# Page gathers of a decoder step issued one by one along the weight half tiles of the first stage; window-cache copies placed in the last stage

## The chip, the cores and the metric

The kernel runs on one core of one Trainium2 chip. The metric is device time in microseconds (us) of one execution. The kernel before took 1522.66 us, the median of three runs (1521.82 to 1527.60).

The engines are PE (TensorE, matmuls, with weight loads shown as PEld), ACT (ScalarE), DVE (VectorE), POOL (GpSimd) and SP (SyncE, here only a DMA queue). Each engine works through its own instructions in order; semaphores order them against each other.

## The reference

One step of a hybrid decoder layer: a half-step feed-forward network, a mixing part with two groups of heads, a second half-step feed-forward network, and a final norm. Prompt (512 rows) and decode rows (8 sequences x 4) go through the same projections. Cut to what matters here:

```python
def ffn_half(x, g, wg, wu, wd):
    h = rms_norm(x, g)
    return x + 0.5 * ((jax.nn.silu(h @ wg) * (h @ wu)) @ wd)

def compress(rows, pe, w1, w2):
    n, length = rows.shape[:2]
    blk = rows.reshape(n, length // CMP_BLOCK, CMP_BLOCK, N_KV_NSA, HEAD_DIM) + pe[:, None, :]
    hid = jnp.einsum('nbcgd,cde->nbge', blk, w1)
    return jax.nn.gelu(hid) @ w2

# in nsa_sample, for the K and the V pool
past = pool[page_table].reshape(n, PAST_LEN, N_KV_NSA, HEAD_DIM)
...
# in reference, for layer l
xp = ffn_half(xp, ffn1_norm[l], ffn1_wg[l], ffn1_wu[l], ffn1_wd[l])
xs = ffn_half(xs, ffn1_norm[l], ffn1_wg[l], ffn1_wu[l], ffn1_wd[l])
...
xp = ffn_half(xp, ffn2_norm[l], ffn2_wg[l], ffn2_wu[l], ffn2_wd[l])
xs = ffn_half(xs, ffn2_norm[l], ffn2_wg[l], ffn2_wu[l], ffn2_wd[l])
# in nsa_sample: the updated window buffers
kw_all = jnp.concatenate([cache_win_k, kw], axis=1)
return ..., kw_all[:, -wb:], vw_all[:, -wb:]
```

D_MODEL is 1024, D_FF 2816. The decode step reads 16 pages of 128 rows for each of 8 sequences, found through a page table: 128 page slots. Each is multiplied by the compression weights w1 (`hid`). The window buffers of the 8 sequences (512 rows) move up by 4 rows, so that 508 rows of each are plain copies.

## The kernel before

The data are f32, and each large product is done as three matmuls on split operands: a weight tile `wraw` gives `wh` (rounded, on ACT) and `wl = wraw - wh` (on DVE), the activations are split likewise (`hh`, `hl`, `ah`, `al`), and PE computes wh x hh, wh x hl and wl x hh. The 544 activation columns are two halves of 272.

**`wload` and the half tiles.** `wload` (around L140) loads a weight tile in pieces of four 128 x 128 blocks (`WK` = 4). Such a piece is called a half tile here: one 256 KB DMA on SP's queue (L148), one conversion on ACT (L150), one subtraction on DVE (L152), then 4 x 3 x 2 = 24 matmuls on PE with 24 weight loads (`dense`, L159). `wraw`, `wh` and `wl` have three buffers each, so a half tile can be prepared while PE is at most three behind.

**The stages.** The first `ffn` runs over 22 f-tiles; each has two half tiles of `wg` and two of `wu`, 96 matmuls in all, and then the silu, the product and the split (L194 to L200). Behind that come eight d with the down projection `wd` in six half tiles each (the last of them half as large), 132 matmuls. Each d ends with squares on ACT (L122) and their sum on POOL (L126) for the next norm. `mix` is the middle stage. The last stage is the second `ffn`, without gathers in it.

**The hook.** The first `ffn` calls `block_step(step)` twice in each f-tile, 44 steps. At f = 3 it computes the gather indices `idx` from the page table. At the steps in `CSTEP` = (8, 15, 22, 29, 36, 43), `block_pages(at)` does two things: the matmuls of the pages fetched at the step before in the list (128 small matmuls of w1 with `cp`, L956, and a copy into `hid`), and then the fetch of the next group (`gather`, L918). A group is 25 or 26 pages (`CG` = 0, 25, 51, 77, 103, 128); for each page POOL issues one indirect DMA of 128 rows. The tile `cp` has one buffer, so a group's gathers wait for the matmuls of the group before. For the first group one more column, the position term `cpe`, is loaded on SP.

**The window copies.** At f = 14 to 21 the hook puts two copies from DRAM to DRAM (254 KB each, L932) on SP's queue between the weight loads, 16 in all. They are kept in program order there.

The order on each engine is set by the tile framework's scheduler from the program order and the dependencies; calls inside `keep_in_program_order` stay in their place.

Of the kernel before, what the change touches and what calls it, by code (L numbers as in the profile page):

```python
# [7 lines left out]
F32 = mybir.dt.float32  # L8
# [10 lines left out]
CG = (0, 25, 51, 77, 103, 128)  # L19
# [4 lines left out]
ZORD = (0, 1, 2, 3, 4, 5, 10, 6, 8, 7, 9)  # L24
KVS = ("kv", "kv", "ar", "hh", "hl")
WB = (3, 3, 3)
CSTEP = (8, 15, 22, 29, 36, 43)
NF = 22
HW = 272
SW = 16  # L30
# [18 lines left out]
class Step:  # L49
# [91 lines left out]
    def wload(self, src, n):  # L141
        nc = self.nc
        out = []
        src = src.rearrange("p (k f) -> p k f", f=128)
        for k0 in range(0, n, WK):
            m = min(WK, n - k0)
            w = self.wp.tile([128, WK, 128], F32, name="wraw", tag="wraw", bufs=WB[0])
            nc.sync.dma_start(w[:, :m], src[:, k0:k0 + m])  # L148
            wh = self.wp.tile([128, WK, 128], F32R, name="wh", tag="wh", bufs=WB[1])
            nc.scalar.activation(wh[:, :m], w[:, :m], AF.Copy)  # L150
            wl = self.wp.tile([128, WK, 128], F32R, name="wl", tag="wl", bufs=WB[2])
            nc.vector.tensor_sub(wl[:, :m], w[:, :m], wh[:, :m].bitcast(F32))  # L152
            out += [(wh[:, j], wl[:, j]) for j in range(m)]
        return out

    def dense(self, p, w, xh, xl, first, last, hs=(0, 1)):
# [182 lines left out]
    def run(self):  # L339
        I, O = self.I, self.O  # L340
        self.setup()
        self.early_w = None
        with ExitStack() as st:
            self.cpool = self.pool("cmp", 1, st)
            self.first_norm()
            self.ffn(I["wg1"], I["wu1"], I["wd1"], I["x"], self.x1, V_MX, self.block_step)
        self.mix()
        self.ffn(I["wg2"], I["wu2"], I["wd2"], self.x2, None, None)
        self.sA.close()

    def mix(self):
# [569 lines left out]
    def block_step(self, step):  # L921
        nc, I, O = self.nc, self.I, self.O
        c = self.cpool
        if step in CSTEP:
            self.block_pages(CSTEP.index(step))
        f = step // 2
        if step % 2:
            return
        if f > 13:
            n = f - 14  # L930
            for o, x in ((O["owk"][n, :, 0:508], I["wkT"][n, :, 4:512]), (O["owv"][n, 0:508], I["wv"][n, 4:512])):
                self.tc.keep_in_program_order(nc.sync.dma_start(o, x))  # L932
        if f == 1:
            self.table_loads()
        if f == 3:
            self.tables()
            self.w1 = c.tile([128, 2, 32, 64], F32, name="w1")
            nc.vector.tensor_copy(self.w1[:, 0, 0, 0:1], self.last[:, 0, 0:1])
            nc.sync.dma_start(self.w1, I["cw1"].rearrange("p (x j e) -> p x j e", x=2, j=32))
            pi = c.tile([128, 128], I32, name="pi")  # L940
            self.tc.keep_in_program_order(nc.sync.dma_start(pi, bass.AP(tensor=I["pt"].tensor, offset=0, ap=[[0, 128], [1, 128]])))
            pf = c.tile([128, 129], F32, name="pf")
            self.tc.keep_in_program_order(nc.sync.dma_start(pf[:, 128:129], I["prow"]))
            nc.vector.tensor_copy(pf[:, 0:128], pi)
            nc.vector.tensor_scalar(self.idx, pf[:, 0:128], 128.0, pf[:, 128:129], op0=OP.mult, op1=OP.add)

    def block_pages(self, at):
        nc, I, c = self.nc, self.I, self.cpool
        if at > 0:
            i = at - 1  # L950
            k0, m = CG[i], CG[i + 1] - CG[i]
            w = 4 * m + (4 if i == 0 else 0)
            ph = self.ps()
            for j in range(32):
                for x in range(2):
                    nc.tensor.matmul(ph[64 * x:64 * x + 64, 0:w], self.w1[:, x, j], self.cp[:, 0:w // 4, x, j], start=j == 0, stop=j == 31)  # L956
            nc.vector.tensor_copy(self.hid[:, 4 * k0:4 * (k0 + m)], ph[:, 0:4 * m])
            if i == 0:
                nc.vector.tensor_copy(self.pb, ph[:, 4 * m:4 * m + 1])
        if at < 5:  # L960
            k0, m = CG[at], CG[at + 1] - CG[at]
            self.cp = c.tile([128, 26, 2, 32, 4], F32, name="cp")
            cf = self.cp.rearrange("p k x j c -> p k (x j c)")
            if at == 0:
                nc.sync.dma_start(cf[:, m], I["cpe"])
            self.gather(cf, I["cmp"], k0, m)

    def mm(self, *args, **kw):
        self.tc.keep_in_program_order(self.nc.tensor.matmul(*args, **kw))  # L969
# [662 lines left out]
```

## Time and profile before

| | |
|---|---|
| median of three runs | 1522.66 us |
| the profiled execution | 1521.93 us |
| its span (first to last instruction) | 1520.1 us |
| DVE busy | 707.0 us (47%) |
| ACT busy | 512.1 us (34%) |
| POOL busy | 250.7 us (16%) |
| page gathers on POOL (L918, cp) | 128, 125.0 us, mean 976 ns |
| window copies on SP (L932) | 16, 254.0 KB each |
| weight half tiles of the first stage's gate and up (L148) | 88 of 256.0 KB |

The table gives what the profile's page says. A page shows the span in 40 equal slices, here of 38 us; a digit is the busy share of a slice in tenths, and the row PEclk is the clock that PE was granted, in tenths of the full one. The chain of work that ended last is followed back from the last instruction, at each step to what released it. "issue" is time in which an engine waited for nothing that the profile shows. In a timeline a row has the start, the length, engine, line, operation, output<-inputs, a count, and in brackets the idle time ahead of it with what ended that. Times are counted from the start of the span.

### The profile page before, as it was taken

The page shows a single profiled execution, that of the slowest core. Times are in us where ns is not written, and L with a number is a line of the kernel's source. Part 1 is how long each engine was busy: PE and PEld are TensorE (multiplying, and loading weights), DVE is VectorE, ACT ScalarE, POOL GpSimd, SP SyncE. Part 2 cuts the span into 40 slices and gives each one's busy share as a digit, 9 for nine tenths or more (in the row PEclk, how much of TensorE's full clock was granted, in tenths as well). Part 3 has the DMA queues.
Part 4 walks back from the last instruction along what each step waited for, and adds up shares of the span by engine and source line. Part 5 has one row for each costly group of instructions (what it writes and reads, how often), then busy time and mean ns, then how long its engine had stood idle before and what let it go on. Part 6 is the DMA issues. An engine that isn't in the chain of part 4 may idle for free.

```text
span 1520.1 us, 31735 instructions
## 1 busy us (share of the span) xinstructions
PE 1367.9 (90%) x13337; PEld 1272.0 (84%) x13337; DVE 707.0 (47%) x1357; ACT 512.1 (34%) x928; POOL 250.7 (16%) x313
## 2 busy tenths in 40 slices
PE   9969686877799999889899986889999999999996
PEld 8969586766799999778776884567999999999996
DVE  6423222222333345694968764457454444443223
ACT  6212121121232236545222334457443333332321
POOL 2153332415100011212000223320100000000100
PEclk9979697978799999997999997889999999999998
DMA  4533333434334342111131564731532222233332
GB/s 158 186 121 102 94 104 107 139 112 139 94 103 119 114 129 86 43 43 39 37 110 29 171 182 149 215 112 44 175 103 89 87 91 86 89 91 106 109 105 84
DMA packets 99329, 163.25 MB, mean 107 GB/s; under 512 B 16186, under 2 KB 42882, under 8 KB 98547
## 3 DMA queue, kind: packets, MB, share of 16 engines
q1 hardware_dynamic: 74978, 116.10, 25.0%
q0 software_dynamic: 9040, 25.24, 5.6%
q10 hardware_dynamic: 15168, 19.89, 4.4%
q8 instruction: 105, 1.72, 0.5%
q14 instruction: 38, 0.30, 0.1%
HBM read 150.19 MB, written 16.72 MB: 110 GB/s over the span
## 4 chain that ended last, share of the span: by engine, by line
PE 80%; issue 7%; DVE 6%; ACT 3%; another core or an unknown queue 1%; DMA 1%; POOL 0%; ACTq 0%; DVEq 0%; SPq 0%; POOLq 0%
PE acc L159 63%; PE pS L969 1%; PE pq L972 1%; PE po L969 1%; PE pp L969 1%; PE pq L714 1%; PE pq L956 1%; PE pp L956 1%; DMA wraw<-in_wg 1%; PE pp L598 1%; PE pp L796 1%; PE pp L497 1%; PE pp L159 1%; DVE ivt L653 0%
## 5 line engine op out<-in xcount | busy, mean ns | idle before, releaser
L159 PE MATMUL acc<-hl,wh 128*128 128x272 f32 x2064 | 437.9, 296 | 27.5 <-issue 26.4
L150 ACT ACTIVATE wh<-wraw 128x512 fp32r<-128x512 f32 x338 | 209.7, 620 | 685.6 <-PE acc L159 507.1
L159 PE MATMUL acc<-hh,wh 128*128 128x272 f32 x1808 | 394.9, 298 | 33.2 <-issue 29.9
L159 PE MATMUL acc<-hh,wl 128*128 128x272 f32 x1808 | 391.8, 297 | 26.0 <-issue 24.4
L152 DVE TENSOR_TENSOR wl<-wraw,wh 128x512 fp32r<-128x512 f32 x338 | 232.5, 688 | 337.4 <-ACT wh L150 279.7
L159 PEld LDWEIGHTS acc<-hl,wh 128*128 128x128 f32 x2064 | 332.0, 194 | 41.0 <-issue 37.2
L159 PEld LDWEIGHTS acc<-hh,wh 128*128 128x128 f32 x1808 | 296.0, 194 | 42.1 <-issue 35.6
L159 PEld LDWEIGHTS acc<-hh,wl 128*128 128x128 f32 x1808 | 293.2, 194 | 33.5 <-issue 30.5
L918 POOL DMA_INDIRECT cp<-in_cmp,idx x128 | 125.0, 976 | 204.6 <-PE pp L956 80.3
L159 PE MATMUL acc<-ah,wh 128*128 128x272 f32 x660 | 137.0, 289 | 0.0
L159 PE MATMUL acc<-al,wh 128*128 128x272 f32 x660 | 136.2, 287 | 0.0
L159 PE MATMUL acc<-ah,wl 128*128 128x272 f32 x660 | 135.5, 286 | 0.0
L126 POOL TENSOR_TENSOR ss<-ss,sq 128x544 f32<-128x544 f32 x23 | 32.0, 1393 | 599.7 <-ACT sq L122 584.3
L159 PEld LDWEIGHTS acc<-al,wh 128*128 128x128 f32 x660 | 104.0, 188 | 0.0
L159 PEld LDWEIGHTS acc<-ah,wl 128*128 128x128 f32 x660 | 103.3, 188 | 0.0
L159 PEld LDWEIGHTS acc<-ah,wh 128*128 128x128 f32 x660 | 102.9, 188 | 0.0
L194 DVE TENSOR_TENSOR t<-acc,r 128x544 f32<-128x544 f32 x42 | 30.4, 724 | 111.3 <-PE acc L159 87.3
L196 DVE TENSOR_TENSOR u<-acc,r 128x544 f32<-128x544 f32 x42 | 30.4, 724 | 108.8 <-PE acc L159 78.5
L918 POOL DMA_INDIRECT kv<-in_slc,idx x36 | 35.5, 986 | 130.1 <-DVE Y L747 64.2
L199 ACT ACTIVATE ah<-u 128x544 fp32r<-128x544 f32 x44 | 29.0, 658 | 65.1 <-DVE u L197 59.3
L200 DVE TENSOR_TENSOR al<-u,ah 128x544 fp32r<-128x544 f32 x44 | 31.9, 725 | 29.0 <-ACT ah L199 28.3
L1416 ACT ACTIVATE ra<-pq 128x512 f32<-128x512 f32 (+2 forms) x48 | 23.7, 521 | 35.9 <-remote 15.4
(515 smaller groups left out, 1482.0 us busy)
## 6 DMA issues: line engine op xcount, KB each, us to landing
wraw<-in_wg SPq DMA_DIRECT2D x88, 256.0 KB
wraw<-in_wu SPq DMA_DIRECT2D x88, 256.0 KB
wraw<-in_wd SPq DMA_DIRECT2D x80, 256.0 KB
wraw<-in_win SPq DMA_DIRECT2D x50, 256.0 KB
kv<-in_slc SPq DMA_DIRECT2D x60, 128.0 KB
x<-xr ACTq DMA_DIRECT2D x16, 272.0 KB
xr<-x ACTq DMA_DIRECT2D x16, 272.0 KB
wraw<-in_wout SPq DMA_DIRECT2D x16, 256.0 KB
```

The lines of the kernel that those rows point to most:

```text
L126: nc.gpsimd.tensor_add(self.ss, self.ss, sq)
L150: nc.scalar.activation(wh[:, :m], w[:, :m], AF.Copy)
L152: nc.vector.tensor_sub(wl[:, :m], w[:, :m], wh[:, :m].bitcast(F32))
L159: self.nc.tensor.matmul(p[h] if isinstance(p, list) else p[:, h, :HW], a, b[:, h], start=f, stop=l)
L194: nc.vector.tensor_mul(t, pt, r)
L196: nc.vector.tensor_mul(u, pu, r)
L199: nc.scalar.activation(ah[:, f], u, AF.Copy)
L200: nc.vector.tensor_sub(al[:, f], u, ah[:, f].bitcast(F32))
L918: self.nc.gpsimd.indirect_dma_start(out=tile[:, k], out_offset=None, in_=rows, in_offset=bass.IndirectOffsetOnAxis(ap=self.idx[:, k0 + k:k ...
L956: nc.tensor.matmul(ph[64 * x:64 * x + 64, 0:w], self.w1[:, x, j], self.cp[:, 0:w // 4, x, j], start=j == 0, stop=j == 31)
L969: self.tc.keep_in_program_order(self.nc.tensor.matmul(*args, **kw))
L1416: self.nc.scalar.activation(t[:, 0:o + w], p[:, 0:o + w], AF.Copy)
```

## The change

`block_pages` becomes a generator. It is made at f = 3, behind the index computation, and kept in `self.pages`. From then on `wload` sends it each half tile's `wh`, right behind the subtraction: all four half tiles of an f-tile, and in the wd loop all six of a d. Each half tile adds `PAGE_RATE` = 1.25 to an account; for each whole unit one page is fetched: first a `tensor_copy` on POOL of one column of `wh` into the place in `cp` that the page will overwrite, and then its gather. The copy makes the gather wait until that half tile has been converted. When a group is complete, the generator lets `PAGE_LAG` = 3 half tiles pass, puts out the group's page matmuls and goes to the next group. The groups themselves are the same. Where the bursts ended at step 36, the pages now run over the rest of the first stage, into the wd loop.

The 16 window copies leave `block_step`. The new hook `window_copies` of the last `ffn` puts one on SP's queue at each of its steps 4 to 19, which are f = 2 to 9.

```diff
@@ -24,7 +24,8 @@
 ZORD = (0, 1, 2, 3, 4, 5, 10, 6, 8, 7, 9)
 KVS = ("kv", "kv", "ar", "hh", "hl")
 WB = (3, 3, 3)
-CSTEP = (8, 15, 22, 29, 36, 43)
+PAGE_RATE = 1.25
+PAGE_LAG = 3
 NF = 22
 HW = 272
 SW = 16
@@ -151,6 +152,8 @@
             wl = self.wp.tile([128, WK, 128], F32R, name="wl", tag="wl", bufs=WB[2])
             nc.vector.tensor_sub(wl[:, :m], w[:, :m], wh[:, :m].bitcast(F32))
             out += [(wh[:, j], wl[:, j]) for j in range(m)]
+            if self.pages:
+                self.pages.send(wh)
         return out
 
     def dense(self, p, w, xh, xl, first, last, hs=(0, 1)):
@@ -339,13 +342,14 @@
     def run(self):
         I, O = self.I, self.O
         self.setup()
-        self.early_w = None
+        self.early_w = self.pages = None
         with ExitStack() as st:
             self.cpool = self.pool("cmp", 1, st)
             self.first_norm()
             self.ffn(I["wg1"], I["wu1"], I["wd1"], I["x"], self.x1, V_MX, self.block_step)
+            assert self.pages is None
         self.mix()
-        self.ffn(I["wg2"], I["wu2"], I["wd2"], self.x2, None, None)
+        self.ffn(I["wg2"], I["wu2"], I["wd2"], self.x2, None, None, self.window_copies)
         self.sA.close()
 
     def mix(self):
@@ -921,15 +925,9 @@
     def block_step(self, step):
         nc, I, O = self.nc, self.I, self.O
         c = self.cpool
-        if step in CSTEP:
-            self.block_pages(CSTEP.index(step))
         f = step // 2
         if step % 2:
             return
-        if f > 13:
-            n = f - 14
-            for o, x in ((O["owk"][n, :, 0:508], I["wkT"][n, :, 4:512]), (O["owv"][n, 0:508], I["wv"][n, 4:512])):
-                self.tc.keep_in_program_order(nc.sync.dma_start(o, x))
         if f == 1:
             self.table_loads()
         if f == 3:
@@ -943,27 +941,44 @@
             self.tc.keep_in_program_order(nc.sync.dma_start(pf[:, 128:129], I["prow"]))
             nc.vector.tensor_copy(pf[:, 0:128], pi)
             nc.vector.tensor_scalar(self.idx, pf[:, 0:128], 128.0, pf[:, 128:129], op0=OP.mult, op1=OP.add)
-
-    def block_pages(self, at):
+            self.pages = self.block_pages()
+            next(self.pages)
+
+    def window_copies(self, step):
+        nc, I, O = self.nc, self.I, self.O
+        n, odd = divmod(step - 4, 2)
+        if 0 <= n < 8:
+            o, x = (O["owv"][n, 0:508], I["wv"][n, 4:512]) if odd else (O["owk"][n, :, 0:508], I["wkT"][n, :, 4:512])
+            self.tc.keep_in_program_order(nc.sync.dma_start(o, x))
+
+    def block_pages(self):
         nc, I, c = self.nc, self.I, self.cpool
-        if at > 0:
-            i = at - 1
+        due, wh = 0.0, (yield)
+        for i in range(len(CG) - 1):
             k0, m = CG[i], CG[i + 1] - CG[i]
+            cp = c.tile([128, 26, 2, 32, 4], F32, name="cp")
+            cf = cp.rearrange("p k x j c -> p k (x j c)")
+            if i == 0:
+                nc.sync.dma_start(cf[:, m], I["cpe"])
+            for k in range(m):
+                while due < 1.0:
+                    wh = yield
+                    due += PAGE_RATE
+                due -= 1.0
+                nc.gpsimd.tensor_copy(cf[:, k, 0:1], wh[:, 0, 0:1].bitcast(F32))
+                self.gather(cf[:, k:k + 1], I["cmp"], k0 + k, 1)
+            for _ in range(PAGE_LAG):
+                yield
             w = 4 * m + (4 if i == 0 else 0)
             ph = self.ps()
             for j in range(32):
                 for x in range(2):
-                    nc.tensor.matmul(ph[64 * x:64 * x + 64, 0:w], self.w1[:, x, j], self.cp[:, 0:w // 4, x, j], start=j == 0, stop=j == 31)
+                    nc.tensor.matmul(ph[64 * x:64 * x + 64, 0:w], self.w1[:, x, j], cp[:, 0:w // 4, x, j], start=j == 0, stop=j == 31)
             nc.vector.tensor_copy(self.hid[:, 4 * k0:4 * (k0 + m)], ph[:, 0:4 * m])
             if i == 0:
                 nc.vector.tensor_copy(self.pb, ph[:, 4 * m:4 * m + 1])
-        if at < 5:
-            k0, m = CG[at], CG[at + 1] - CG[at]
-            self.cp = c.tile([128, 26, 2, 32, 4], F32, name="cp")
-            cf = self.cp.rearrange("p k x j c -> p k (x j c)")
-            if at == 0:
-                nc.sync.dma_start(cf[:, m], I["cpe"])
-            self.gather(cf, I["cmp"], k0, m)
+        self.pages = None
+        yield
 
     def mm(self, *args, **kw):
         self.tc.keep_in_program_order(self.nc.tensor.matmul(*args, **kw))
```

On POOL, in the first stage, before: the table loads (`tbl`, `rvd`, `tbd`, `rvr`), and then all page gathers, a group held back only by the page matmuls of the one before.

```order
L294 DMA rvd<-tbl 8x383
L314 DMA tbd<-tbl 128x448
L296 DMA rvr<-rvd 128x3064
L918 DMA cp<-in_cmp,idx 128x256 x128
L469 DMA ident<-in_ident 128x128
```

The same place now; `wh` is the converted half tile.

```order
L297 DMA rvd<-tbl 8x383
L317 DMA tbd<-tbl 128x448
L299 DMA rvr<-rvd 128x3064
L968 COPY cp<-wh 128x1 x5
L922 DMA cp<-in_cmp,idx 128x256 x5
L968 COPY cp<-wh 128x1 x2
L922 DMA cp<-in_cmp,idx 128x256 x2
L968 COPY cp<-wh 128x1
L922 DMA cp<-in_cmp,idx 128x256
L968 COPY cp<-wh 128x1 x2
L922 DMA cp<-in_cmp,idx 128x256 x2
```

The first five pages stand together, those after them singly or in pairs, each behind a copy from its half tile. In the wd loop the sum of squares of a d (L127) stands among them, one for each d:

```order
L127 TENSOR_TENSOR ss<-ss,sq 128x544
L968 COPY cp<-wh 128x1
L922 DMA cp<-in_cmp,idx 128x256
L968 COPY cp<-wh 128x1 x2
L922 DMA cp<-in_cmp,idx 128x256 x2
L968 COPY cp<-wh 128x1
L922 DMA cp<-in_cmp,idx 128x256
L968 COPY cp<-wh 128x1
L922 DMA cp<-in_cmp,idx 128x256
L968 COPY cp<-wh 128x1
L922 DMA cp<-in_cmp,idx 128x256
L968 COPY cp<-wh 128x1 x2
```

On ACT, in f-tile 3 and 4 after the change, with the engines that each instruction waits for: the conversions of half tiles (L151, before L150) now wait for POOL too, whose copy must have read the buffer's former content.

```order
L151 ACTIVATE wh<-wraw 128x512 [waits DMAHW0_49,PE_49,Activation_49]
L198 ACTIVATE t<-t 128x544 [waits DVE_49]
L151 ACTIVATE wh<-wraw 128x512 [waits DMAHW1_49,PE_49,Pool_49]
L151 ACTIVATE wh<-wraw 128x512 [waits DMAHW6_49,PE_49,Pool_49]
L151 ACTIVATE wh<-wraw 128x512 [waits DMAHW7_49,PE_49,Pool_49]
L202 ACTIVATE ah<-u 128x544 [waits DVE_49]
```

The page matmuls on PE move with the groups: the first three blocks stand in the gate and up loop, the fourth and fifth in the wd loop (behind d = 2 and d = 6), where before all five stood in the gate and up loop.

## The prediction

> **What bounds the kernel now.** I read the page first: shares, the slices, the chain and the costliest groups.
>
> ```profile
> PE 1367.9 (90%) x13337; PEld 1272.0 (84%) x13337; DVE 707.0 (47%) x1357; ACT 512.1 (34%) x928; POOL 250.7 (16%) x313
> PE   9969686877799999889899986889999999999996
> PEclk9979697978799999997999997889999999999998
> PE 80%; issue 7%; DVE 6%; ACT 3%; another core or an unknown queue 1%; DMA 1%; POOL 0%; ACTq 0%; DVEq 0%; SPq 0%; POOLq 0%
> ```
>
> TensorE is the bound, and every matmul has a weight load (both x13337). But a slice is 38 us, and slices 3 to 12, the gate and up loop of the first stage, show PE at 6 to 8 and a granted clock at 6 to 8, while the same loop in the last stage shows 9 and 9. The chain gives 7% of the span to "issue", waiting for nothing that the profile shows. So I asked for the waits of PE in that loop, and for the windows around one burst of page gathers.
>
> ```profile
> PE acc L159 <- issue: 80.7, 79, 2.4
> PE acc L159 <- ACT wh L150: 0.6, 1, 0.6
> ```
>
> Between 70.2 and 434.6 us PE waits 0.6 us for a weight half tile and 80.7 us for "issue", so neither the weights nor the page data are late.
>
> ```profile
> 136.00:146.00 10.00, 10.00 (x82) 10.00 (x81) 3.48 (x7) 1.92 (x3) 7.85 (x8) 1.00 0.46 138
> 146.00:156.00 10.00, 4.60 (x25) 3.36 (x23) 0.69 (x1) 0.63 (x1) 7.57 (x9) 0.86 0.44 127
> 156.00:166.00 10.00, 3.37 (x8) 2.46 (x9) 0.00 (x0) 0.00 (x0) 7.57 (x9) 0.50 0.39 110
> 166.00:176.00 10.00, 5.05 (x18) 4.19 (x18) 2.05 (x3) 1.81 (x3) 2.08 (x3) 0.50 0.21 63
> 70.20:434.60 364.40, 282.19 (x2361) 267.80 (x2362) 100.06 (x155) 71.47 (x112) 126.50 (x133) 0.83 0.38 112
> 1134.90:1375.40 240.50, 240.50 (x1922) 240.50 (x1922) 107.84 (x161) 76.92 (x120) 0.00 (x0) 1.00 0.29 90
> ```
>
> The columns are window, length, then PE, weight loads, DVE, ACT, POOL as busy time with instructions, granted clock, DMA share, GB/s. The second burst starts at 136. For ten microseconds PE runs on at full clock; in the next twenty it starts 33 matmuls, where the last stage starts 160 (1922 in 240.5 us, 8.0 per us); the clock falls to 0.50. DMA is under half busy throughout. The timelines of POOL and of PE show the two sides.
>
> ```profile
> 136.02 0.94 POOL L918 DMA_INDIRECT cp<-in_cmp,idx  x1 [33.18 <-PE pq L956]
> 137.27 0.95 POOL L918 DMA_INDIRECT cp<-in_cmp,idx  x1 [0.30 <-issue]
> ...
> 167.75 0.95 POOL L918 DMA_INDIRECT cp<-in_cmp,idx  x1 [0.30 <-issue]
> ```
> ```profile
> 104.91 0.29 PEld L159 LDWEIGHTS acc<-hh,wl 128*128 128x128 f32 x1 [1.11 <-issue]
> 105.61 0.39 PE L159 MATMUL acc<-hh,wl 128*128 128x272 f32 x1 [1.01 <-issue]
> ```
> ```profile
> 129.88 5.86 PE pq L956 x128
> 135.74 11.47 PE acc L159 x90
> ...
> 172.68 29.79 PE acc L159 x220
> ```
>
> Gathers leave POOL every 1.25 us. Late in the first burst PE gets one instruction per 0.70 us. In the second it executes 90 matmuls and 90 loads after the burst begins (chain row 135.74: a **reserve of 180 instructions**), crawls, and runs freely again at 172.68, 4.93 us after the last gather's start. I read this as: while POOL works on a gather, PE's instructions are hardly supplied, and PE lives on its reserve. A second place supports it.
>
> ```profile
> 869.71 1.89 POOL L1324 COPY bias<-t 128x2048 f32<-128x2048 f32 x1
> 874.78 0.94 POOL L918 DMA_INDIRECT kv<-in_slc,idx  x1 [0.71 <-remote]
> ```
> ```profile
> 870.19 3.20 PE L1258 MATMUL pp<-px,w1r 128*64 128x16 f32 x90
> 873.80 0.42 PE L1258 MATMUL pp<-px,w1r 128*64 128x16 f32 x4 [0.42 <-issue]
> 874.53 2.44 PE L1258 MATMUL pp<-px,w1r 128*64 128x16 f32 x34 [0.30 <-issue]
> ```
>
> PE pauses while gathers run, and takes up 34 matmuls with their loads when POOL is free for 0.71 us ahead of the gather at 874.78. The plain copy of 1.89 us holds nothing up.
>
> **The change, part by part.** The profiled execution took 1521.9 us, 1.8 us more than its span and 0.05% under the median of the runs; the sum is made against it.
>
> *The bursts go.* Their price is the loop's time less what it would need. The rows that start each f-tile's last product mark it.
>
> ```profile
> 69.44 0.73 DVE L197 TENSOR_TENSOR u<-u,t 128x544 f32<-128x544 f32 x1
> 433.95 0.72 DVE L197 TENSOR_TENSOR u<-u,t 128x544 f32<-128x544 f32 x1
> 1134.25 0.72 DVE L197 TENSOR_TENSOR u<-u,t 128x544 f32<-128x544 f32 x1
> 1374.71 0.72 DVE L197 TENSOR_TENSOR u<-u,t 128x544 f32<-128x544 f32 x1
> ```
>
> f-tile 3 to 21 of the first stage: 364.51 us for 18 tiles. Tile 1 to 21 of the last stage, without gathers: 240.46 us for 20, or 12.02 each. 18 x 12.02 = 216.4; five blocks of page matmuls at 5.86 (row 129.88) are 29.3; the excess is 364.5 - 216.4 - 29.3 = **118.8 us**. The waits agree: 80.7 us of issue, and the rest is matmuls at half clock (PE busy 282.2 against 245.7 needed).
>
> *What one gather holds up, B.* Not below its 0.95 us on POOL; not above 4.93 us, as if the whole tail of the burst were one gather's. The nearest estimate is the mean: from 136.02 to 172.68 are 36.66 us for 26 gathers, 1.41 each; I take **1.41**. While one holds, PE gets 1.7 instructions per us (17 in window 156:166). Between, it gets at least 44 per us: the page matmuls drew 256 in 5.86 us without starving, and the gap at 874 suggests more.
>
> *The new spacing.* Each four half tiles of weights, 12.02 us of PE work with 192 instructions, release five gathers, two of them as a pair. Held: 4 x 1.41 + 1.25 = 6.9 us; free: 5.1 us, which admits 5.1 x 44 = 225, over 192. In the wd loop one d has 132 matmuls, 16.5 us at 8.0 per us, 264 instructions and 7.5 gathers: held 6 x 1.41 + 1.5 x 1.25 = 10.3, free 6.2, which admits 271, and 17 come during the holds. So PE should not starve in either, and the reserve of 180 covers the opening five back to back (6.3 us) and each pair. The margin lasts to B = 1.68 in the f loop and 1.51 in wd; with more than 44 per us it is wider. This cover is the whole gain: without it the price is in the rivals.
>
> *The copies from wh.* 128 new POOL copies of one column. The nearest rows:
>
> ```profile
> L489 POOL COPY sho<-zp 128x1 f32<-128x1 f32 x14 | 4.0, 287 | 0.0
> L619 POOL COPY pcs<-prep 128x8 f32<-128x8 f32 x1 | 0.7, 706 | 0.0
> L152 DVE TENSOR_TENSOR wl<-wraw,wh 128x512 fp32r<-128x512 f32 x338 | 232.5, 688 | 337.4 <-ACT wh L150 279.7
> L126 POOL TENSOR_TENSOR ss<-ss,sq 128x544 f32<-128x544 f32 x23 | 32.0, 1393 | 599.7 <-ACT sq L122 584.3
> ```
>
> At 0.29 us a d costs POOL 7.5 x (1.25 + 0.29) + 1.39 for the sum of squares = 12.9 of 16.5 us; at 0.71 us 16.1. Both fit, so POOL keeps pace. Between these ends I take 0.29, the same shape.
>
> The Trainium skill, GPSIMD Engine Reference, section 1 (Specifications), says that GpSimd shares its SBUF interfaces with VectorE and contends with DVE instructions that have two SBUF inputs. Such are the wl subtractions, one per half tile. The gathers at 0.94 to 0.95 us beside a working DVE don't show it; by the rule a copy could be held for one subtraction, and the sum would be that of the third rival.
>
> *New wait on ACT.* The conversion of half tile n+3 now also waits until POOL has copied from n. Queued behind it on ACT are the later conversions, the silu and the ah splits; PE waits for all of them. Below nothing it can't go, since nothing is taken from ACT. As price I take one wait per page group like the single one that PE had for a conversion:
>
> ```profile
> 70.61 0.52 PE L159 MATMUL acc<-hh,wh 128*128 128x272 f32 x2 [0.62 <-ACT wh L150]
> ```
>
> 5 x 0.62 = **3.1 us**; the ends are 0 and 3.1.
>
> *Page matmuls moved.* Still five blocks of 5.86 us, two of them now in the wd loop: 0. The bias-adding column, the gelu of hid and its table load come in d = 7, ahead of readers at 857 us: 0. The identity load on POOL waits for the last page block as before, and its first reader comes after the first stage.
>
> *Window copies.* Sixteen DRAM to DRAM copies leave SP's queue between weight loads of f 14 to 21 and enter it in f 2 to 9 of the last stage, one per half step. Where they are now, they cost PE nothing:
>
> ```profile
> 400.00:430.00 30.00, 30.00 (x324) 29.73 (x323) 11.44 (x20) 9.81 (x15) 2.00 (x5) 1.00 0.37 103
> out_owk<-in_wkT SPq DMA_DIRECT2D x8, 254.0 KB
> ```
>
> PE is full there at clock 1.00 with a DMA share of 0.37. In the last stage the share is 0.29 (window row above), so 0 there too. The cover is the weights' three half tiles ahead, 9 us of PE work; if it were gone, each copy would delay a load by the time that 254 KB take at 103 GB/s, 2.5 us: 16 x 2.5 = 40, so the ends are 0 and 40, and I take 0 from the window row.
>
> Sum: 1521.9 - 118.8 + 3.1 = **1406 us**. Best case without the new wait 1403.
>
> **The rivals.**
>
> *(a) PE still starves in part.* If B is not 1.41 but 1.95 (the longest single gather in the trace), four half tiles take 13.06 us instead of 12.02, and a d 19.05 instead of 16.5: held 9.05, then (192 - 15) / 44 = 4.0; held 13.6, then (264 - 23) / 44 = 5.5. About 84 gathers fall in the f loop (16.8 groups of five) and 44 in wd (5.9 d): 17.5 + 15.3 = 33 us, so **1439**.
>
> ```profile
> L918 POOL DMA_INDIRECT cp<-in_cmp,idx x128: 942/946/1502, 69.6 to 384.5; - x128
> L918 POOL DMA_INDIRECT kv<-in_slc,idx x36: 940/947/1951, 854.2 to 1018.3; - x36
> ```
>
> For it: the margin in wd is thin. Against it: these rows of line 918 (shortest, median and longest in ns) have the median at 0.95, and the gap at 874 admitted 68 instructions in 0.71 us, far over 44 per us.
>
> *(b) The slower side: a gather holds PE for its whole tail.* The mechanism is the 4.93 us from the last gather's start to PE's recovery. If all of that belongs to each gather and bursts merely let the tails overlap, spacing them exposes every tail. Four half tiles then take 24.5 us, a d 36.2: 16.8 x 12.5 + 5.9 x 19.7 = 326 us, **1732**. It turns slower at B = 2.8, where the same formula returns about 117 us. For it speaks only the tail; against it, PE resuming in a 0.71 us gap at 874.53.
>
> *(c) POOL becomes the bound in wd.* If each copy is held for one wl subtraction (0.69 + 0.29 = 0.98 us), a d needs 7.5 x 2.23 + 1.39 = 18.1 us on POOL, 1.6 over; 5.9 x 1.6 = 9.5: **1416**.
>
> *(d) The spacing doesn't happen.* The scheduler could put gathers in bursts after all: about **1522**. The instruction order speaks against it: copies and gathers alternate.
>
> **How the numbers follow.** Forecast 0.70, (a) 0.18, (b) 0.05, (c) 0.04, (d) 0.03. The range runs from 1401 (all excess gone, no new wait, and 2 us for the spread of runs) to 1446 (the copies' other end), which takes in (c) and (a) at 1439; what lies over it is the upper half of (a), (b) and (d), 0.17. A measurement of this kernel can tell about 0.5% from no change. Faster: forecast, (a), (c), 0.92; same: (d), 0.03; slower: (b), 0.05.
>
> **What would show it.** Right: in the f loop PE waits for issue near 0 instead of 80.7 us; clock 1.00 in every window from 70 to 430; 12.02 us per f-tile and 16.5 per d, plus 5.86 where a page block stands; gathers in singles and pairs. Wrong by (a): small issue waits after pairs and clock under 1.00, first in wd. By (b): an issue wait after every gather. By (c): in wd, ACT's conversions waiting for POOL, with copies near 1 us. By (d): gathers every 1.25 us over tens of us. The forecast fails if a gather's hold on PE doesn't end with the gather.

## The result, and the profile after

The changed kernel took **1406.13 us**, the median of four runs (1401.62 to 1407.38), against 1523.03 us for the kernel before (four runs): a ratio of 0.922 (95% interval 0.919 to 0.925). Its profiled execution took 1406.21 us, with a span of 1404.4, 115.7 us less than before.

The page of the changed kernel: busy slices, granted clock, the chain, and the groups of gathers (L922, before L918) and copies (L968, new).

```profile
PE   8999999999999998889999777899999999999996
PEclk9999999999999998799899998999999999999998
PE 81%; DVE 7%; issue 4%; ACT 3%; DMA 2%; another core or an unknown queue 1%; POOL 1%; ACTq 0%; SPq 0%; DVEq 0%; POOLq 0%
L922 POOL DMA_INDIRECT cp<-in_cmp,idx x128 | 128.9, 1007 | 44.0 <-POOL cp L968 25.0
L968 POOL COPY cp<-wh 128x1 f32<-128x1 f32 x128 | 53.5, 430 | 118.5 <-ACT wh L151 62.4
```

Slices 3 to 12 now show 9 throughout, and the clock with them. (Before, PE stood at 6 to 8 in eight of these ten slices and the clock in six; the prediction's "6 to 8" for all of them reads too much, but its sum doesn't use it.) The gathers are as many as before and nearly as long (mean 1007 ns, before 976); what differs is their places. The windows of the changed kernel, with the same columns as in the prediction, and the waits of PE from 70.2 to 434.6 us:

```profile
70.20:434.60 364.40, 361.47 (x3270) 358.67 (x3270) 143.06 (x211) 104.82 (x167) 189.13 (x257) 1.00 0.47 140
1030.00:1270.00 240.00, 240.00 (x1918) 240.00 (x1917) 106.64 (x159) 75.59 (x120) 0.00 (x0) 1.00 0.33 102
```
```profile
PE acc L162 <- issue: 1.9, 5, 0.6
PE acc L162 <- ACT wh L151: 1.0, 1, 1.0
```

Issue waits fell from 80.7 to 1.9 us; PE runs 3270 matmuls in a window in which it ran 2361, at clock 1.00. In the last stage, which now has the window copies, PE is still full (240.00 of 240.00), with a DMA share of 0.33 where it was 0.29. What is left of the stall stands at the opening, in the chain of waits and on POOL:

```profile
71.92 10.89 PE acc L162 x83
...
85.94 1.03 PE acc L162 x5
86.97 0.42 issue
87.39 39.34 PE acc L162 x312
126.73 5.86 PE pq L976 x128
132.59 72.35 PE acc L162 x576
```
```profile
71.44 1.44 POOL L922 DMA_INDIRECT cp<-in_cmp,idx  x1 [5.38 <-DVE u L199]
73.18 0.97 POOL L922 DMA_INDIRECT cp<-in_cmp,idx  x1 [0.30 <-issue]
...
85.44 0.98 POOL L922 DMA_INDIRECT cp<-in_cmp,idx  x1 [0.27 <-issue]
```

Eleven gathers stand close together from 71.44 to 85.44, and PE crawls from 82.81 to 87.39: the old stall in small. From then on six f-tiles (576 matmuls) take 72.35 us, 12.06 each, with gathers among them.

### The profile page after: what moved, and what is told of

Its sections match the earlier page's. It is cut to its first block, busy times and chain, and to the rows that moved or that the text cites. A ratio compares the mean times of both kernels' runs of the same rounds, so it can differ in the third digit from the quotient of the medians.

```text
span 1404.4 us, 31989 instructions
## 1 busy us (share of the span) xinstructions
PE 1332.2 (95%) x13337; PEld 1247.6 (89%) x13337; DVE 709.3 (51%) x1357; ACT 512.7 (37%) x928; POOL 309.3 (22%) x441
## 4 chain that ended last, share of the span: by engine, by line
PE 81%; DVE 7%; issue 4%; ACT 3%; DMA 2%; another core or an unknown queue 1%; POOL 1%; ACTq 0%; SPq 0%; DVEq 0%; POOLq 0%
PE acc L162 63%; PE po L984 1%; PE pq L987 1%; PE pS L984 1%; PE pp L984 1%; PE pq L718 1%; PE pq L976 1%; DMA wraw<-in_wg 1%; PE pp L602 1%; PE pp L976 1%; PE pp L800 1%; DMA tbd<-tbl 1%; PE pp L162 1%; ACT Sp L1408 1%
## 5 line engine op out<-in xcount | busy, mean ns | idle before, releaser
L162 PE MATMUL acc<-hl,wh 128*128 128x272 f32 x2064 | 427.7, 292 | 1.4 <-ACT on L1446 0.7
L151 ACT ACTIVATE wh<-wraw 128x512 fp32r<-128x512 f32 x338 | 209.7, 621 | 570.0 <-PE acc L162 509.9
L162 PE MATMUL acc<-hh,wh 128*128 128x272 f32 x1808 | 384.7, 293 | 5.3 <-ACT wh L151 1.7
L162 PE MATMUL acc<-hh,wl 128*128 128x272 f32 x1808 | 381.9, 292 | 1.4 <-DVE wl L153 1.1
L162 PEld LDWEIGHTS acc<-hl,wh 128*128 128x128 f32 x2064 | 324.3, 190 | 9.1 <-issue 5.3
L162 PEld LDWEIGHTS acc<-hh,wh 128*128 128x128 f32 x1808 | 288.2, 190 | 11.9 <-issue 6.0
L162 PEld LDWEIGHTS acc<-hh,wl 128*128 128x128 f32 x1808 | 285.7, 190 | 5.7 <-issue 2.7
L127 POOL TENSOR_TENSOR ss<-ss,sq 128x544 f32<-128x544 f32 x23 | 32.1, 1395 | 510.9 <-ACT sq L123 494.9
L922 POOL DMA_INDIRECT cp<-in_cmp,idx x128 | 128.9, 1007 | 44.0 <-POOL cp L968 25.0
L968 POOL COPY cp<-wh 128x1 f32<-128x1 f32 x128 | 53.5, 430 | 118.5 <-ACT wh L151 62.4
L922 POOL DMA_INDIRECT kv<-in_slc,idx x36 | 36.1, 1004 | 128.1 <-DVE Y L751 64.3
```

Source lines behind the costliest of these rows:

```text
L127: nc.gpsimd.tensor_add(self.ss, self.ss, sq)
L162: self.nc.tensor.matmul(p[h] if isinstance(p, list) else p[:, h, :HW], a, b[:, h], start=f, stop=l)
L922: self.nc.gpsimd.indirect_dma_start(out=tile[:, k], out_offset=None, in_=rows, in_offset=bass.IndirectOffsetOnAxis(ap=self.idx[:, k0 + k:k ...
L968: nc.gpsimd.tensor_copy(cf[:, k, 0:1], wh[:, 0, 0:1].bitcast(F32))
```

## The experiments

Twelve runs, four jobs. Each job has a chip of its own, which its results number, and runs of the kernel before on that chip. Diffs are against the changed kernel unless said otherwise.

**Job 1, chip 14: bursts in the changed kernel's frame.** The pages of a group are released in one, two or three bursts at the same mean rate; the credit also grows while the page matmuls are awaited. The diff is that of whole groups; two parts have a lag of 7, three a lag of 6.

```diff
-PAGE_LAG = 3
+PAGE_LAG = 13
+PAGE_PARTS = 1
...
+            cut = [m * j // PAGE_PARTS for j in range(PAGE_PARTS + 1)]
...
-                while due < 1.0:
-                    wh = yield
-                    due += PAGE_RATE
-                due -= 1.0
+                if k in cut:
+                    n = cut[cut.index(k) + 1] - k
+                    while due < n:
+                        wh = yield
+                        due += PAGE_RATE
+                    due -= n
```

Whole groups:

> The changed kernel, but each group of 25 or 26 pages is released at once when its credit is complete, at the same mean rate, with the copies from the half tiles and the window copies in the last stage kept; the page matmuls follow 13 half tiles later. Theory (a gather holds PE's supply for about 1.41 us and PE lives on a reserve of 180 instructions): each burst of 26 costs as before, 5 x 23.8 = 119 us over a kernel without stalls (1403): about 1522. Rival (the gain came from the release by weight tiles, or from where the pages and copies stand): about 1406.

Halves:

> As the run with whole groups, but in bursts of 12 or 13, page matmuls 7 half tiles later. Theory: a burst of 13 holds for 18.3 us, in which PE needs 293 instructions and has 180 of reserve and 31 that get through; 82 are missing, 5.1 us, ten times: 1403 + 51 + 5 for the fallen clock, about 1460. Rival (stalls grow with the number of gathers, without a reserve): half of 119, or as much as whole groups: 1522. Rival (release by weight tiles decides): 1406.

Thirds:

> As before, in bursts of 8 or 9, page matmuls 6 half tiles later. Theory: a burst of 9 holds for 12.7 us, needs 203 instructions, has 180 + 22: no stall, 1403 to 1410. Rival (PE's reserve is only the few us that a queue of 64 would give): 203 - 64 - 22 = 117 missing, 7.3 us, 15 times: about 1510.

Whole groups with gaps (on top of the diff above, `PAGE_LAG` = 20; the gathers are kept in program order too):

```diff
+                self.tc.keep_in_program_order(nc.gpsimd.memset(self.gap, 0.0))
                 self.gather(cf[:, k:k + 1], I["cmp"], k0 + k, 1)
```

> Whole groups released at once, as in the first of these runs, but with a POOL memset of 128x512 ahead of each gather, kept in program order, so that the gathers of a burst stand about 2.2 us apart by POOL's own work; the page matmuls follow 20 half tiles later. Theory (only the spacing counts): of 2.2 us 0.8 are free, which admit 35 instructions, and PE needs 35: no or small stalls, 1406 to 1430. Rival (the release by the weight tiles counts, or the number of gathers in a burst): about 1520.

Measured: 1371.6, 1365.0, 1367.0 and 1475.3 us. But on this chip **the kernel before itself took 1367.0 us** (18 runs, 1361.3 to 1375.8), so that the first three are within 0.4% of it (1.004, 0.998, 1.001), and no theory's number applies. One window inside a burst of the first of them shows why:

```profile
130.00:150.00 20.00, 20.00 (x162) 20.00 (x162) 8.58 (x14) 7.07 (x11) 13.70 (x14) 1.00 0.60 184
70.00:430.00 360.00, 355.75 (x3202) 354.18 (x3204) 137.50 (x205) 102.35 (x163) 163.75 (x261) 1.00 0.46 139
```

POOL issues gathers back to back, most of them 1.25 us apart, and PE runs full beside them at clock 1.00. Here a gather holds nothing. The fourth run was slow for another reason: all 25 or 26 copies of a group read one half tile, the last of them some 45 us after the first, so that its buffer stayed taken.

```profile
PE acc L163 <- ACT wh L152: 99.4, 7, 20.3
```

What follows: the stall isn't a matter of the instruction stream alone. So the next job took the two kernels themselves along.

**Job 2, chip 3: both kernels again, and whole groups and thirds again.**

The kernel before, unchanged:

> The kernel before, unchanged, with a profile of its own on this chip. In the job ahead of this one it took 1367 us in 18 runs where 1523 was measured at first, and bursts of 26 gathers stalled nothing. Theory (the hold of PE during gathers belongs to the chip on which a run lands): either about 1523 with five stalls of 24 us, or about 1367 with PE at full clock through the bursts, and nothing between. Rival (it varies from execution to execution on one chip): runs of both kinds in this job.

The changed kernel, unchanged:

> The changed kernel, unchanged. Theory: on a chip that holds PE, about 1406; on one that doesn't, the first stage has no stall to lose and the change is worth nothing: within 1% of the kernel before there, about 1367. Rival (the change's structure itself costs or saves something): over 1% from the kernel before on a chip without holds.

Whole groups:

> Whole groups of 25 or 26 released at once, in the changed kernel's frame. Theory: as the kernel before on the same chip: about 1522 with holds, 1370 without. Rival: 1406 with holds (the release by weight tiles decides).

Thirds:

> Bursts of 8 or 9. Theory: with holds 1403 to 1410, since PE's reserve covers a burst of 9; without holds as the kernel before, 1367. Rival (a reserve of 64): with holds about 1510.

Measured: 1528.6, 1411.8, 1529.5 and 1422.1 us, with the kernel before at 1529.8 (15 runs, 1525.0 to 1535.3); the ratios of the last three are 0.920 (0.918 to 0.923), 0.9995 (0.997 to 1.002) and 0.927 (0.924 to 0.930). By their times, every execution of the kernel before and of whole groups on this chip (1522 to 1537 us) holds PE, as none on chip 14 did. The window from 70 to 430 us in the four kernels, in that order:

```profile
70.00:430.00 360.00, 268.00 (x2223) 255.55 (x2223) 98.02 (x149) 68.89 (x108) 124.60 (x128) 0.82 0.36 112
```
```profile
70.00:430.00 360.00, 357.37 (x3169) 355.10 (x3169) 140.11 (x207) 102.56 (x165) 185.81 (x255) 1.00 0.46 140
```
```profile
70.00:430.00 360.00, 293.73 (x2359) 283.68 (x2359) 108.52 (x164) 78.22 (x123) 118.80 (x205) 0.86 0.32 102
```
```profile
70.00:430.00 360.00, 350.50 (x3145) 345.07 (x3143) 132.53 (x203) 99.13 (x159) 161.47 (x265) 1.00 0.44 134
```

Whole groups bring the whole loss back, although they keep the copies from the half tiles, the places of the pages up to the burst, and the window copies in the last stage: those parts are worth nothing by themselves; the spacing is. (In the window a part of the loss is missing, because these bursts run on into the wd loop, behind 430 us.) Bursts of 8 or 9 cost 1422.1 - 1411.8 = 10.4 us over the changed kernel, 0.7 us for each of 15 bursts, where my theory said none and a reserve of 64 would have cost 7.3 us each. So, if a gather holds PE for 1.41 us, the reserve is near 180, a little below. The waits of PE in the thirds show these small ends of bursts; the changed kernel has 2.6 us of them on this chip:

```profile
PE acc L163 <- issue: 8.8, 18, 1.1
```

**Job 3, chip 10: spacing without half tiles, and other ways to fetch.** Whole groups once more with gaps, now with one copy for each group:

```diff
-                nc.gpsimd.tensor_copy(cf[:, k, 0:1], wh[:, 0, 0:1].bitcast(F32))
+                if k in cut:
+                    nc.gpsimd.tensor_copy(cf[:, k, 0:1], wh[:, 0, 0:1].bitcast(F32))
+                self.tc.keep_in_program_order(nc.gpsimd.memset(self.gap, 0.0))
```

> Whole groups of 25 or 26 released at once by one copy, with a POOL memset of 128x768 ahead of each gather, in program order: the gathers of a burst stand about 1.95 us apart by POOL's own work alone. (In the run with gaps before, each page's copy read the same half tile, which kept its buffer: PE waited 99 us for conversions.) On a chip with holds: theory (only the spacing counts): 0.54 of 1.95 us free admits 24 instructions and 2 get through, 31 are needed, and the reserve of 180 covers the 5 x 26 missing: few stalls, 1406 to 1430. Rival (the number of gathers in a burst, or the release by the weights, counts): about 1525. On a chip without holds: as the kernel before.

The kernel before with plain DMAs on POOL (diff against the kernel before):

```diff
-            self.gather(cf, I["cmp"], k0, m)
+            for k in range(m):
+                nc.gpsimd.dma_start(cf[:, k], I["cmp"][k0 + k])
```

> The kernel before with its five bursts, but POOL fetches the pages by plain DMAs, page n in place of the page that the table names (the table is left out for the compressed pages). On a chip with holds: theory (POOL's work of issuing a DMA holds PE): the issue waits of PE stay, in proportion to POOL's time for each, 0.5 to 1.0 us: 1440 to 1530. Rival (only the indirect form holds): issue wait near 2 us, about 1410.

The same with `nc.sync.dma_start`:

> The same pages in the same bursts, fetched by plain DMAs on SP's queue (the table is left out for them too). On a chip with holds: theory (POOL's work holds PE, not the pages' traffic): issue wait near 2 us; since a burst's 3.3 MB stand ahead of weight loads, PE may wait up to 10 us per burst for conversions: 1405 to 1460. Rival (the traffic holds PE's supply): issue waits of 80 us as before, 1520 or more.

Measured: 1409.2 us (0.920, 0.917 to 0.924), 1405.1 us (0.918, 0.914 to 0.921) and 1423.5 us (0.930, 0.922 to 0.937), with the kernel before at 1532.0: a chip that holds. POOL in the first of them, and PE from 70 to 430 us:

```profile
140.81 1.36 POOL L923 DMA_INDIRECT cp<-in_cmp,idx  x1 [0.16 <-issue]
142.17 0.75 POOL L977 MEMSET gap<- 128x768 f32 x1
143.08 1.18 POOL L923 DMA_INDIRECT cp<-in_cmp,idx  x1 [0.16 <-issue]
```
```profile
70.00:430.00 360.00, 360.00 (x3192) 358.88 (x3191) 140.49 (x208) 104.14 (x166) 235.29 (x264) 1.00 0.46 141
```

Groups of 25 or 26 gathers, some 2 us apart with 0.75 us of memset between, leave no issue wait. That settles that the spacing works by itself, whatever makes it, and that POOL being busy (235.29 of 360 us) doesn't hold PE. The SP run has no issue wait from 60 to 450 us, so the traffic doesn't hold PE either; it lost time to weight loads queued behind pages:

```profile
PE pq L956 <- DMA wraw<-in_wu: 11.1, 1, 11.1
PE acc L159 <- ACT wh L150: 1.6, 1, 1.6
```

The plain POOL DMAs didn't stall PE, against my theory; but at 0.54 us each a burst lasts 14 us, little more than the reserve. Hence the last run.

**Job 4, chip 1: plain POOL DMAs for as long as a burst of gathers.** Against the kernel before:

```diff
-            self.gather(cf, I["cmp"], k0, m)
+            for k in range(m):
+                for c0 in (0, 128):
+                    nc.gpsimd.dma_start(cf[:, k, c0:c0 + 128], I["cmp"][k0 + k, :, c0:c0 + 128])
```

> As the bursts of plain POOL DMAs (page n in place of the table's), but each page in two halves, so that a burst of 52 DMAs at 0.54 us keeps POOL for about 28 us, as long as a burst of gathers; with whole pages it was 14 us, not far over PE's reserve of 11 us, and PE lost nothing. Theory (any DMA that POOL issues holds PE for POOL's time): 28 us x 16 = 448 instructions needed, 180 + 48 there, 220 missing, 14 us per burst: about 1475, with 40 us or more of issue waits. Rival (only the indirect form holds PE): issue waits near 2 us, about 1406. On a chip without holds both give about 1367 and nothing is told apart.

Measured: 1404.7 us (0.922, 0.918 to 0.926), with the kernel before at 1524.0, so this chip holds as well. The second burst on POOL, the windows in it, and the waits of PE from 60 to 450 us:

```profile
118.48 27.34 POOL L968 DMA_DIRECT2D cp<-in_cmp  x52 [22.67 <-PE pq L956]
```
```profile
120.00:130.00 10.00, 10.00 (x82) 10.00 (x82) 4.07 (x6) 2.55 (x4) 10.00 (x20) 1.00 0.63 176
130.00:140.00 10.00, 10.00 (x82) 10.00 (x81) 4.78 (x8) 3.85 (x6) 10.00 (x20) 1.00 0.71 222
140.00:150.00 10.00, 10.00 (x82) 10.00 (x81) 4.14 (x7) 2.56 (x4) 5.83 (x12) 1.00 0.58 176
```
```profile
PE acc L159 <- ACT wh L150: 1.2, 1, 1.2
```

POOL issues DMAs without a pause for 27.34 us, with DMA shares of 0.58 to 0.71, over those of a gather burst, and PE starts 246 matmuls in 30 us, as many as it can. Of the forms tried, only the indirect one holds PE. What in an indirect DMA does it, and how it reaches PE's instructions, no run shows.

With the page table in place, no run on a chip that holds PE was faster than the changed kernel; the run with gaps, 1409.2 us on chip 10, was not compared with it on one chip.

## Why the prediction was right, step by step

*The bursts' price, 118.8 us.* Right. The rows of the changed kernel that answer to those of f-tile 3 and 21:

```profile
71.22 0.72 DVE L200 TENSOR_TENSOR u<-u,t 128x544 f32<-128x544 f32 x1
308.54 0.72 DVE L200 TENSOR_TENSOR u<-u,t 128x544 f32<-128x544 f32 x1
```

These are 237.3 us, with three of the page blocks between them: 216.4 + 3 x 5.86 = 234.0 would do, so an excess of 3.3 us is left of 118.8. That gives 115.5; the loop begins 1.8 us later than before, and some 2 us come back behind it, 115.7 in all. The prediction had neither of these two; that they cancel is luck.

*The new wait on ACT, 3.1 us.* Right in size by luck, wrong as a cause. PE lost 1.0 us in this loop to a conversion, once, and that conversion had waited for its weight DMA and not for POOL. The wait from which the price was taken (row 70.61 of the kernel before) was of the same kind. The conversion and the wait after the change, and the conversion before it:

```profile
71.24 1.32 ACT L151 ACTIVATE wh<-wraw 128x512 fp32r<-128x512 f32 x2 [6.06 <-DMA wraw<-in_wg]
71.92 0.52 PE L162 MATMUL acc<-hh,wh 128*128 128x272 f32 x2 [1.04 <-ACT wh L151]
```
```profile
69.93 1.31 ACT L150 ACTIVATE wh<-wraw 128x512 fp32r<-128x512 f32 x2 [7.49 <-DMA wraw<-in_wg]
```

ACT waited for POOL's copies twice, 1.6 us in all, and PE shows no wait from it: the term was nearer 0. What it happened to cover is the opening, which the prediction put at nothing. I had read five gathers back to back out of the order of instructions, and let the reserve cover them. But POOL waited for DVE until 71.44 us (first gather's row) while the half tiles went on giving credit, so eleven gathers came close together; eleven at 1.41 us need 248 instructions, more than the reserve, and PE crawled.

*B = 1.41 us, and 44 instructions per us between gathers.* Borne out as a mean: a spacing of some 2 us by memsets and the pairs of the changed kernel starve nothing, and in wd, where the margin was said to be thin, there is no issue wait. Neither figure was measured by itself.

*The reserve of 180.* Nearly right: bursts of 8 or 9 should have been free and cost 0.7 us each, some 11 instructions.

*The mechanism.* Half right. That PE is held, that nothing it waits for is late, and that spacing cures it were shown, by the return of the loss with whole groups and by its absence with gaps. "While POOL works on a gather" was too wide in one way: POOL's DMAs as such don't hold PE, only the indirect ones. And it left out what no trace of one chip could show, that another chip doesn't hold PE at all; that the result was taken where PE is held was luck, for on a chip like 14 there was nothing to gain.

*The copies.* Taken at 0.29 us, they took 0.43 in the mean (row of line 968), under the 0.71 that was still to fit; POOL didn't become the bound. Their length follows DVE's subtractions:

```profile
88.16 0.69 DVE L153 TENSOR_TENSOR wl<-wraw,wh 128x512 fp32r<-128x512 f32 x1
88.19 0.71 POOL L968 COPY cp<-wh 128x1 f32<-128x1 f32 x1 [1.78 <-ACT wh L151]
95.68 0.19 POOL L968 COPY cp<-wh 128x1 f32<-128x1 f32 x1
```

Of the 37 copies that began with no product or subtraction of DVE beside them, 36 took 0.18 to 0.21 us. All 65 copies that began while a wl subtraction ran ended 0.04 to 0.05 us after it. Beside products that read one input from PSUM (lines 197 and 199) 24 copies took 0.18 to 0.19 us. So the rule of the Trainium skill that the prediction cites (GPSIMD Engine Reference, section 1, Specifications) holds here: a copy is held by a DVE instruction with two inputs in SBUF. But (c) priced it too high, at 0.98 us: the longest took 0.71, because the wait for the subtraction is most of it.

*Window copies, page blocks in wd.* 0 and 0, as said; the chain shows each page block with its 5.86 us and PE full around it.

*Rivals.* (a), partial starving, happened only at the opening. (In its price the second term is 5.9 x 2.55 = 15.0, not 15.3; 1439 stands.) (b), the whole tail for each gather, would have given 1732. (c) and (d) didn't occur. The forecast of 1406 therefore held in both places where the changed kernel ran (1406 and, on chip 3, 1412), and both hold PE. On chip 14 the changed kernel itself was not run; that there was nothing to gain is read from the thirds, at 1.001 of the kernel before.

## What to carry to other kernels

When an engine idles for "issue", waiting for nothing that the profile shows, look at what other engines issue in that stretch; here the cure was to spread 128 indirect DMAs so that the engine's reserve of instructions never ran out. How the spacing is made doesn't matter, a dependence or filler work; what a burst may hold up is the reserve (here some 170 instructions by the thirds, 11 us at PE's pace). And measure a gain on more than one chip before counting on it: the same kernel had a stall worth 8% on one and none on another.

## What the runs showed of the hardware

- **Chips differ.** The kernel before took 1367.0 us on chip 14 and 1524.0 to 1532.0 us on chips 1, 3 and 10, each time in all its runs. On chip 14 a gather takes POOL as long, 0.95 us and mostly 1.25 us from start to start, and PE runs on. Why they differ stays open: nothing in the traces names it, and since each numbered chip was seen in one job alone, something else about the job isn't ruled out.
- **The middle stage differs too.** From the end of the first stage's work to the long run of 480 matmuls, whole groups need 1070.16 - 577.10 = 493.1 us on chip 3 and 909.02 - 458.19 = 450.8 us on chip 14; the changed kernel, on a chip that holds, needs 944.02 - 457.20 = 486.8. Of the 42 us between the first two, 158 - 122 = 36 lie in one stretch, which has 39 of the 48 indirect gathers of this stage. In it PE waits 11.2 us for "issue" on chip 3 and not at all on chip 14. So the gathers may well cost PE here too; a run that spaces or replaces them was not tried.

The stretch in whole groups, on chip 3 and on chip 14, in the columns of the prediction's windows:

```profile
912.20:1070.20 158.00, 124.19 (x1399) 95.47 (x1398) 87.43 (x337) 84.77 (x240) 38.44 (x42) 0.87 0.43 132
```
```profile
787.00:909.00 122.00, 111.26 (x1398) 87.06 (x1397) 88.02 (x337) 84.25 (x240) 38.94 (x42) 0.99 0.56 171
```

- **A plain DMA costs POOL 0.54 us, an indirect one 0.98** (means of 256 half pages and of the 128 gathers before), and of the two only the second held PE, on the chips where anything did.
- **A small POOL copy beside a DVE instruction with two SBUF inputs is held to its end** (0.71 against 0.18 us; rows under the copies above).
